# Output projections of both cross attentions as 2x2 block products with seven multiplications

## The chip, the core and the metric

The kernel runs on one core of one Trainium2 chip. Five engines work side by side, each through its own queue: TensorE (PE, with its weight loads PEld), VectorE (DVE), ScalarE (ACT), GpSimd (POOL) and SyncE (SP). The metric is the device time of one execution in microseconds; the kernel before takes 2214.82 us (median of three runs, 2214.09 to 2217.98).

## The reference

A trunk of two layers on 1024 tokens of 1024 features, float32. A layer is a token mixer (Fourier groups and neighbourhood attention in layer 0, a gated short convolution in layer 1), a cross attention into 256 memory tokens, and a gated ConvFFN. The change lies in the last line of the cross attention and in the residual addition:

```python
def memory_cross_attention(h, m, wq, wkv, wo):
    ...
    q = (h @ wq).reshape(B, S, XA_HEADS, XA_HEAD_DIM)
    ...
    p = jax.nn.softmax(s, axis=-1).astype(v.dtype)
    o = jnp.einsum('bhsm,bmhd->bshd', p, v).reshape(B, S, D)
    return o @ wo

    # in reference(), for each of the two layers, after the mixer:
    h = h + memory_cross_attention(rms_norm(h, xa_norm_g[layer]), m,
                                   xa_wq[layer], xa_wkv[layer], xa_wo[layer])
    h = h + conv_ffn(rms_norm(h, ffn_norm_g[layer]), ...)
```

## The kernel before

Activations stand transposed, features on partitions and tokens on the free axis. h is eight tiles of 128 features x 1024 tokens; chunk 0 and chunk 1 are its token halves of 512. Float32 products are made from float32r ones: an operand is split into a high part (ACT, `nc.scalar.copy`, L222) and a low part (DVE, a subtraction, L223), and `mm3` (L227 to L229) issues three matmuls into one PSUM bank. `wide_split` splits 1024 columns into two places, `half_split` 512 columns into one. SBUF is 52 places of 1024 columns and four half places of 512, handed out by `alloc`; a free half place is preferred for an allocation of 512 columns, and among free ones that which was freed longest ago.

The work is written as generators (threads) that `run` interleaves by a share of progress; each thread has a length in the call. The instruction order on each engine is fixed when the kernel is built, and need not be that of the text: what is ready early is put early.

`xattn(l, st)` is the cross attention. `qproj(c)` makes the queries of chunk c. `attn` goes over eight (chunk, head) pairs: `scores`, softmax, transposes (`turn`), then `values`, whose PSUM result is split with `half_split` into `os_`. `oproj(c)` is the output projection of chunk c through `linear`: eight blocks of 128 outputs, eight k each, weights `wo` loaded from DRAM by SP (L250) and split. `res_post` adds a block into h on DVE (L813), squares it on ACT (`sumsq`, L314) and adds up the squares on DVE (L320). The first run is `qproj(0)` alone; then `qproj(1)` and `oproj(0)` run beside `attn`; then `oproj(1)` runs alone, with `xb0` (the FFN's operands of chunk 0: `rstd`, `xnorm` L1111, `wide_split`) as a hook.

The up projection, the down projections and the convolution mixer's projections are already block products with seven multiplications. An item there is a weight block pair; of its seven weight operands three lie in DRAM as they are, and four are sums (products 7, 6, 5 and 3). `plan_sums` lists the sums to be made, and each call of `sums(src)` starts the next one of the list, whatever item it belongs to: ACT copies one element of `src` into `gates` (L1071), and POOL issues three DMAs, the gate into the target (L1072), the first operand into it (L1073), and the second one with accumulation (L1074). Each of the three writes the target and waits for the one before to land. `w_load` and `w_prep` load and split a weight operand; `plan_steps` lists them as tasks, and `ahead(n, keep)` does up to n tasks while there is room.

`down` is such a projection with a residual: products 1, 6 and 7 leave temporaries (L1474 to L1490), and product by product the results are added to or subtracted from h on DVE. CHAIN says which PSUM chain a product belongs to, OPENS and ENDS where a chain begins and ends. In `up_steps`, the FFN's operands of chunk 1 (`xb1`) follow as a background generator that `pump` moves.

The number of calls of `sums` is 136, that of sums too: 56 calls in the mixer of layer 0 (32 in its input projection, 16 and 8 in its output projections), 16 in each cross attention (four in each `qproj`, four in each `oproj`), 24 in the first up projection, 6 in the first down projection, 12 and 6 in layer 1's mixer.

Of the kernel before, what the change touches and what calls it, by code (L numbers as in the profile page):

```python
# [10 lines left out]
F32 = mybir.dt.float32  # L11
F32R = mybir.dt.float32r
AF = mybir.ActivationFunctionType
ALU = mybir.AluOpType
# [4 lines left out]
KT = 8  # L19
# [14 lines left out]
HK = 3  # L34
HU = 3
PF = 8
AW = 55.0
GATES = 64
KEEP = 8
KEEPD = 6  # L40
# [2 lines left out]
U = 512  # L43
# [85 lines left out]
class Kern:  # L129
    def __init__(self, ctx, tc, ap):  # L130
        self.tc, self.nc, self.ap = tc, tc.nc, ap
        nc = self.nc
# [25 lines left out]
        self.dr = dr  # L158
        self.q, self.did, self.op, self.xd, self.hd, self.wsrc = [], set(), {}, {}, {}, {}
        self.bg = None  # L160
        self.gates = sb.tile([P, GATES], F32, name="gates")
        self.nsum = 0

# [659 lines left out]

    def mixer0(self):
        nc = self.nc
        self.plan_sums([*self.up_items(0), *self.down_items("d0", 2, self.ap["w_down"][0]), *self.conv_items(),
                        *self.down_items("oc", 1, self.ap["w_out_c"]), *self.up_items(1),
                        *self.down_items("d1", 2, self.ap["w_down"][1])])
        self.z, self.yf, self.qkv = {}, {}, {}
        self.done = set()  # L830
# [32 lines left out]
    def xattn(self, l, st):  # L863
        nc = self.nc
        qs = [{}, {}]
        os_ = [{}, {}]
        qdone = [-1, -1]

        def qproj(c, hooks=()):
# [22 lines left out]
        def attn():  # L892
# [47 lines left out]
            def values(hd):  # L940
                h, kv, pp = hd["h"], hd["kv"], hd["p"]
                for db in range(2):
                    b = yield from self.bank(1)
                    for j in range(2):
                        self.mm3(b.f(), *self.hl(kv[1], j * NM + db * P, P), *self.wcols([pp], j * U, U),
                                 j == 0, j == 1)
                    os_[hd["c"]][2 * h + db] = yield from self.half_split(b.f())
                    self.bfree(b)
                    yield 1.3
                self.free(*pp, *kv)  # L950

            prev = nxt = ready = None
            for n in range(18):
# [20 lines left out]

        st2 = {}

        def oproj(c, hooks=()):
            psum, post = self.res_post(st2)
            while len(os_[c]) < KT:
                yield None  # L980

            def X(k, cc):
                return self.hl(os_[c][k])
            yield from self.linear([(b, c) for b in range(KT)], self.ap["wo"][l], KT, X, psum, post,
                                   hooks=hooks)
            self.free(*os_[c].values())

        self.run((qproj(0, [((0, HU), lambda: self.normed(G_XA + 8 * l, st, 1))]), 41.0))

        def main():  # L990
            yield from qproj(1)
            yield from oproj(0)
        self.run((main(), 83.0), (attn(), AW))
        self.run((oproj(1, [((0, HU), lambda: self.xb0(G_FFN + 8 * l, st2))]), 41.0))
        return st2


    def conv3(self, tmp, src, w, bias):
# [598 lines left out]
    def all(self):  # L1597
        self.run((self.warm(), 1.0))
        self.run((self.mem_load(), 1.0))

        def kv():
            yield from self.kv_thread(0)
            yield from self.kv_thread(1)
        self.run((self.x_norm(), XW), (kv(), 86.0))
        self.wfree(self.m)
        st = self.mixer0()
        self.plan_up(0)
        self.plan_down("d0", 2)
        self.plan_conv()
        self.plan_down("oc", 1)  # L1610
        st = self.xattn(0, st)
        st = self.trunk(st)
        self.plan_up(1)
        self.plan_down("d1", 2)
        st = self.xattn(1, st)
        self.last(st)
# [80 lines left out]
def prepare(x, mem, mem_norm_g, mix_norm_g, w_in_ab, rpb, w_out_ab, w_in_c, conv_c, w_out_c,  # L1697
# [18 lines left out]
    def downs(w):  # L1716
# [7 lines left out]
        "wk": np.stack([_blocks(xa_wkv[l][:, :D]) for l in range(2)]),  # L1724
        "wv": np.stack([_cols(xa_wkv[l][:, D:], 256) for l in range(2)]),
        "wq": np.stack([_blocks(xa_wq[l]) for l in range(2)]),
        "wo": np.stack([_blocks(xa_wo[l]) for l in range(2)]),
        "w_up": np.stack(up), "w_down": np.stack([downs(ffn_w_down[l]) for l in range(2)]),
        "w_cc": cc, "w_cb": cb, "w_out_c": downs(w_out_c[0]),
    }  # L1730
# [20 lines left out]
```

## Time and profile before

| | us |
|---|---|
| median of three runs | 2214.82 |
| the profiled execution, whole | 2223.45 |
| its span, first to last instruction | 2221.7 |
| PE busy | 2166.7 |
| DVE busy | 1459.9 |
| ACT busy | 960.0 |
| POOL busy | 342.4 |

Busy times are those of the profiled execution and are read against its span. PE's granted clock is 0.989 of full speed over the span. The first cross attention lies at about 460 to 675 us, the second at about 1500 to 1735 us, with the up projections right behind. A row that ends in "<-" names what ended the idle time before an instruction.

### The profile page before, as it was taken

To read this page: it belongs to the slowest core of one execution; us is meant where nothing else is said; L and a number is where in the kernel's file an instruction comes from. 1 tells how busy PE (TensorE), PEld (TensorE's weight loads), DVE (VectorE), ACT (ScalarE), POOL (GpSimd) and SP (SyncE) were. 2 spreads that over 40 slices of the span, in tenths; PEclk is the share of its full clock that TensorE was granted. 3 is DMA by queue.
4 is the path that set the end of the run, shared out by engine and by line. 5 is a ranking of instruction groups with operands and counts; after the bars stand their busy time and mean duration, and the time that the engine had idled before them with its cause. 6 is when DMAs were issued, how large, how long until landed. Compare 5 with 4: busy or idle time off the path is not lost.

```text
span 2221.7 us, 27033 instructions
## 1 busy us (share of the span) xinstructions
PE 2166.7 (98%) x10174; PEld 1788.3 (80%) x10174; DVE 1459.9 (66%) x2001; ACT 960.0 (43%) x1498; POOL 342.4 (15%) x446
## 2 busy tenths in 40 slices
PE   9999999999998999999999999999999999999998
PEld 9988888888886777777888878778888777888887
DVE  6755456666667576666767667777565757767684
ACT  6543444355445334344445223535444533334553
POOL 5222222222211221111101100011111000000002
PEclk9999999999999999999999999999999999999999
DMA  9467787789877678999874666965666635446652
GB/s 371 152 164 176 159 210 202 187 230 228 218 193 206 166 209 222 254 289 338 266 218 135 182 194 188 341 171 143 173 168 178 172 110 163 146 152 247 259 176 76
DMA packets 177891, 446.11 MB, mean 201 GB/s; under 512 B 19808, under 2 KB 87648, under 8 KB 175584
## 3 DMA queue, kind: packets, MB, share of 16 engines
q1 hardware_dynamic: 101344, 310.14, 39.6%
q0 software_dynamic: 76416, 134.25, 29.6%
q8 instruction: 79, 1.29, 0.2%
q14 instruction: 52, 0.43, 0.1%
HBM read 386.64 MB, written 191.89 MB: 260 GB/s over the span
## 4 chain that ended last, share of the span: by engine, by line
PE 81%; DMA 8%; DVE 8%; ACT 2%; issue 1%; DVEq 0%; SPq 0%; ACTq 0%
PE PS L228 27%; PE PS L227 26%; PE PS L229 26%; DMA xd_d<-p 3%; DVE p L223 2%; ACT p L222 1%; DMA p<-ws_u 1%; DMA p<-in_w_down_dram 1%; DMA xd_oc<-p 1%; PE PS L932 1%; DMA p<-in_wq_dram 1%; DVE p L1006 1%; DVE p L1008 1%; DMA p<-xd_d 0%; PE PS L695 0%
## 5 line engine op out<-in xcount | busy, mean ns | idle before, releaser
L227 PE MATMUL PS<-p,p 128*128 128x512 f32 (+1 forms) x3264 | 1225.0, 380 | 36.1 <-ACT p L222 28.4
L228 PE MATMUL PS<-p,p 128*128 128x512 f32 (+1 forms) x3264 | 1234.1, 379 | 5.1 <-DVE p L223 4.9
L229 PE MATMUL PS<-p,p 128*128 128x512 f32 (+1 forms) x3264 | 1219.5, 377 | 2.3 <-DVE p L223 2.3
L223 DVE TENSOR_TENSOR p<-p,p 128x1024 fp32r<-128x1024 f32 (+1 forms) x549 | 607.2, 1126 | 279.6 <-ACT p L222 218.9
L222 ACT CAST p<-p 128x1024 fp32r<-128x1024 f32 (+1 forms) x566 | 529.6, 959 | 571.1 <-DMA p<-xd_d 89.6
L227 PEld LDWEIGHTS PS<-p,p 128*128 128x128 f32 x3264 | 617.6, 189 | 165.9 <-ACT p L222 36.0
L228 PEld LDWEIGHTS PS<-p,p 128*128 128x128 f32 x3264 | 617.6, 189 | 125.6 <-DVE p L223 7.0
L229 PEld LDWEIGHTS PS<-p,p 128*128 128x128 f32 x3264 | 616.4, 189 | 123.3 <-DVE p L223 2.9
L314 ACT ACTIVATE p<-p 128x512 f32<-128x512 f32 (+1 forms) x128 | 74.3, 589 | 101.5 <-DVE p L813 41.8
L320 DVE TENSOR_TENSOR p<-p,p 128x512 f32<-128x512 f32 (+1 forms) x111 | 79.9, 722 | 31.4 <-ACT p L314 28.8
L223 DVE TENSOR_TENSOR p<-PS,p 128x512 fp32r<-128x512 f32 (+3 forms) x92 | 67.7, 744 | 41.3 <-ACT p L222 41.0
L1589 POOL TENSOR_TENSOR p<-p,p 128x512 f32<-128x512 f32 (+1 forms) x15 | 16.4, 1125 | 451.5 <-DVE p L494 433.7
L222 ACT CAST p<-PS 128x512 fp32r<-128x512 f32 (+3 forms) x92 | 57.3, 631 | 52.1 <-PE PS L229 28.4
L1072 POOL DMA_DIRECT2D ws_u<-gates x64 | 42.6, 756 | 241.4 <-ACT gates L1071 241.3
L813 DVE TENSOR_TENSOR p<-PS,p 128x512 f32<-128x512 f32 x64 | 43.8, 687 | 48.7 <-PE PS L229 48.7
L1005 ACT ACTIVATE p<-p,vec 128x1024 f32<-128x1024 f32 x32 | 39.7, 1242 | 66.4 <-DVE p L1305 53.6
L1006 DVE SCALAR_TENSOR_TENSOR p<-p,vec,p 128x1023 f32<-128x1023 f32 x40 | 51.2, 1281 | 20.0 <-ACT p L1005 18.4
L1074 POOL DMA_DIRECT2D ws_u<-ws_u x32 | 33.3, 1040 | 201.4 <-DMA ws_u<-in_w_up_dram 113.3
L1073 POOL DMA_DIRECT2D ws_u<-in_w_up_dram x64 | 36.9, 591 | 163.4 <-DMA ws_u<-gates 163.1
L1071 ACT COPY gates<-p 128x1 f32<-128x1 f32 x136 | 24.6, 191 | 74.1 <-DVE p L813 33.5
L1074 POOL DMA_DIRECT2D ws_u<-in_w_up_dram x32 | 33.6, 1050 | 133.7 <-DMA ws_u<-in_w_up_dram 94.9
L1300 DVE TENSOR_TENSOR p<-PS,p 128x512 f32<-128x512 f32 x32 | 22.0, 688 | 48.1 <-PE PS L229 48.0
(170 smaller groups left out, 1308.9 us busy)
## 6 DMA issues: line engine op xcount, KB each, us to landing
ws_u<-in_w_up_dram POOLq DMA_DIRECT2D x96, 512.0 KB, 5.8
p<-ws_u SPq DMA_DIRECT2D x64, 512.0 KB, 4.5
xd_d<-p SPq DMA_DIRECT2D x112, 256.0 KB, 6.0
p<-xd_d SPq DMA_DIRECT2D x56, 512.0 KB, 6.4
ws_d<-in_w_down_dram POOLq DMA_DIRECT2D x48, 512.0 KB, 6.4
p<-in_w_up_dram SPq DMA_DIRECT2D x48, 512.0 KB, 4.5
ws_u<-ws_u POOLq DMA_DIRECT2D x32, 512.0 KB, 6.2
p<-in_wq_dram SPq DMA_DIRECT2D x32, 512.0 KB, 4.5
```

What stands on the lines that cost most here:

```text
L222: self.nc.scalar.copy(hi, src)
L223: (eng or self.nc.vector).tensor_tensor(lo, src, hi.bitcast(F32), op=ALU.subtract)
L227: mm(ps, whi, xhi, start=first, stop=False, skip_group_check=True)
L228: mm(ps, whi, xlo, start=False, stop=False, skip_group_check=True)
L229: mm(ps, wlo, xhi, start=False, stop=last, skip_group_check=True)
L314: nc.scalar.activation(t.f(0, w), src, AF.Square)
L320: nc.vector.tensor_tensor(st[ch].f(0, w), st[ch].f(0, w), t.f(0, w), op=ALU.add)
L813: self.nc.vector.tensor_tensor(hc, ps, hc, op=ALU.add)
L1005: nc.scalar.activation(tmp.f(), src, AF.Identity, scale=v[:, w[1]:w[1] + 1], bias=v[:, bias:bias + 1])
L1006: nc.vector.scalar_tensor_tensor(tmp.f(1, S), src[:, 0:S - 1], v[:, w[0]:w[0] + 1], tmp.f(1, S), op0=ALU.mult, op1=ALU.add)
L1072: g.dma_start(d[0:1, 0:1], gate[0:1])
L1074: g.dma_start(d, more, accum_op=ALU.add, max_dma_last_dim=1024)
```

## The change

The output projection becomes one block product over both chunks. The 1024 x 1024 matrix `wo` and the attention's output (features by tokens) are each taken as 2 x 2 blocks of 512, and the four result blocks come from seven block products in place of eight. `values` copies its PSUM result on ACT into a raw place, two halves to a place. `o_operands` makes the seven operands from the raw places on DVE as the heads come in: operands 1 and 2 (chunk 0's blocks as they are) beside the attention, 5 and 6 with chunk 1's heads, and 7, 4 and 3 through the background generator `o_rest`. `oproj` runs in the thread of `qproj(1)`: products 1 and 2 of both couples first, then 6, 7, 4, 5, 3. The main thread's length goes from 83 to 122 and the attention's (AW) from 55 to 105.

The residual steps are those of `down`, but where `down` uses DVE to apply the temporaries of products 1, 6 and 7 to h, the new function uses `nc.gpsimd.tensor_tensor` (`pt`): twelve such steps in a layer. Two calls of `sums` stand at each of products 1, 6 and 7, one for each couple: six in a layer in place of eight. The weights of `wo` become two items per layer with four sums each; layer 0's eight are put first in the list, layer 1's ahead of the second up projection's. `xb0` starts behind product 4 of the second couple. Four hooks in `qproj(1)` load and split the first weight operands.

```diff
-AW = 55.0
+AW = 105.0
...
-        self.plan_sums([*self.up_items(0), *self.down_items("d0", 2, self.ap["w_down"][0]), *self.conv_items(),
-                        *self.down_items("oc", 1, self.ap["w_out_c"]), *self.up_items(1),
+        self.plan_sums([*self.down_items("o0", 1, self.ap["wo"][0]), *self.up_items(0), *self.down_items("d0", 2, self.ap["w_down"][0]), *self.conv_items(),
+                        *self.down_items("oc", 1, self.ap["w_out_c"]),
+                        *self.down_items("o1", 1, self.ap["wo"][1]), *self.up_items(1),
                         *self.down_items("d1", 2, self.ap["w_down"][1])])
...
-                    os_[hd["c"]][2 * h + db] = yield from self.half_split(b.f())
+                    if db == 0:
+                        r = yield from self.alloc(F32)
+                    nc.scalar.copy(r.f(db * U, (db + 1) * U), b.f())
                     self.bfree(b)
                     yield 1.3
                 self.free(*pp, *kv)
+                yield from self.o_operands(hd["c"], h, r)
...
-        def oproj(c, hooks=()):
-            psum, post = self.res_post(st2)
...
         def main():
-            yield from qproj(1)
-            yield from oproj(0)
-        self.run((main(), 83.0), (attn(), AW))
-        self.run((oproj(1, [((0, HU), lambda: self.xb0(G_FFN + 8 * l, st2))]), 41.0))
+            yield from qproj(1, [((i, 0), lambda: self.ahead(2, KEEP)) for i in (4, 5, 6, 7)])
+            yield from self.oproj("o%d" % l, st2, lambda: self.xb0(G_FFN + 8 * l, st2))
+        self.run((main(), 44.0 + 78.0), (attn(), AW))
         return st2
+
+    ORDO = ((1, 0), (2, 0), (1, 1), (2, 1)) + tuple((p, c) for p in (6, 7, 4, 5, 3) for c in range(2))
+
+    def o_operands(self, c, h, r):
+        tt = self.nc.vector.tensor_tensor
+        m = h % 2
+        half = h // 2
+        raw = self.oraw
+
+        def whole(p, x):
+            self.O.setdefault(p, []).append((yield from self.wide_split(x.f())))
+
+        if c == 0:
+            raw[half, m] = r
+            yield from whole(1 + half, r)
+        elif half == 0:
+            raw[2, m] = r
+            t1 = raw[0, m]
+            tt(t1.f(), t1.f(), r.f(), op=ALU.subtract)
+            yield from whole(5, t1)
+        else:
+            t1 = raw[0, m]
+            tt(t1.f(), r.f(), t1.f(), op=ALU.add)
+            yield from whole(6, t1)
+            raw[3, m] = r
+            if m == 1:
+                self.bg = self.o_rest()
+
+    def o_rest(self):
+        tt = self.nc.vector.tensor_tensor
+        for p, i, j in ((7, 2, 3), (4, 1, 0), (3, 3, None)):
+            for m in range(2):
+                x = self.oraw[i, m]
+                if j is not None:
+                    tt(x.f(), x.f(), self.oraw[j, m].f(), op=ALU.subtract)
+                self.O.setdefault(p, []).append((yield from self.wide_split(x.f())))
+                self.free(x)
+                if j == 0:
+                    self.free(self.oraw[0, m])
+                yield 1.0
...
+    def oproj(self, tag, st2, after):
+        nc = self.nc
+        bk, t1s, half = {}, {}, set()
+        tt, pt = nc.vector.tensor_tensor, nc.gpsimd.tensor_tensor
+
+        def done(k, c):
+            yield from self.sumsq(st2, c, k, self.hch(k, c))
+
+        def post(c, q, p, bank):
+            i, j = COUPLES[c][q]
+            b = bank.f()
+            if p == 1:
+                t1 = t1s[c, q] = yield from self.alloc(F32, 1)
+                nc.scalar.copy(t1.f(0, U), b)
+                if q == 0:
+                    self.sums(t1.f(0, 1))
+                pt(self.hch(j, 0), self.hch(j, 0), t1.f(0, U), op=ALU.subtract)
+            elif p == 6:
+                t2 = yield from self.alloc(F32, 1)
+                tt(t2.f(0, U), b, t1s[c, q].f(0, U), op=ALU.subtract)
+                if q == 0:
+                    self.sums(t2.f(0, 1))
+                pt(self.hch(i, 1), self.hch(i, 1), t2.f(0, U), op=ALU.subtract)
+                self.free(t2)
+            elif p == 7:
+                t1 = t1s.pop((c, q))
+                tt(t1.f(0, U), b, t1.f(0, U), op=ALU.subtract)
+                if q == 0:
+                    self.sums(t1.f(0, 1))
+                pt(self.hch(j, 1), self.hch(j, 1), t1.f(0, U), op=ALU.add)
+                self.free(t1)
+            elif p in (2, 4):
+                k = i if p == 2 else j
+                tt(self.hch(k, 0), b, self.hch(k, 0), op=ALU.add)
+                yield from done(k, 0)
+            elif p == 5:
+                tt(self.hch(j, 1), self.hch(j, 1), b, op=ALU.subtract)
+            else:
+                tt(self.hch(i, 1), self.hch(i, 1), b, op=ALU.add)
+                yield from done(i, 1)
+            if p in (5, 7):
+                if (c, q) in half:
+                    yield from done(j, 1)
+                half.add((c, q))
...
+            if (p, c) == (4, 1):
+                yield from self.pump()
+                self.bg = after()
+            yield from self.pump(3 if p in (5, 3) else 1)
+            yield from self.ahead(4, KEEP)
+        yield from self.pump()
...
-        "wo": np.stack([_blocks(xa_wo[l]) for l in range(2)]),
+        "wo": np.stack([downs(xa_wo[l]) for l in range(2)]),
```

## Rows read from the trace of the kernel before

**Rows 1.** The page, part 1: busy us, share of the span, instructions.

```profile
PE 2166.7 (98%) x10174; PEld 1788.3 (80%) x10174; DVE 1459.9 (66%) x2001; ACT 960.0 (43%) x1498; POOL 342.4 (15%) x446
```

**Rows 2.** Timeline of PE (start, us, instruction): first and last of twelve.

```profile
439.75 0.40 PE L227 MATMUL PS<-p,p 128*128 128x512 f32 x1
...
442.31 0.39 PE L229 MATMUL PS<-p,p 128*128 128x512 f32 x1
```

**Rows 3.** Busy time by stretch: engines with count, PE clock, DMA share, GB/s.

```profile
500.00:612.00 112.00, 112.00 (x593) 95.20 (x593) 68.96 (x119) 53.48 (x118) 25.99 (x36) 1.00 0.89 222
612.00:672.00 60.00, 60.00 (x261) 48.41 (x260) 34.56 (x44) 22.91 (x33) 10.36 (x15) 1.00 0.77 203
672.00:716.00 44.00, 37.54 (x156) 29.50 (x155) 36.46 (x38) 28.06 (x40) 7.29 (x11) 0.94 0.77 195
...
1728.00:1773.00 45.00, 41.12 (x168) 32.23 (x167) 36.99 (x38) 27.60 (x37) 3.61 (x5) 0.96 0.56 159
```

**Rows 4.** Busy time of L1071 (ACT), then of L1072 (POOL), from the start.

```profile
0.00:485.00 485.00, 10.13 (x59) 0.99 0.75 205
0.00:631.00 631.00, 11.67 (x67) 0.99 0.77 208
...
0.00:485.00 485.00, 31.88 (x43) 0.99 0.75 205
0.00:631.00 631.00, 44.75 (x59) 0.99 0.77 208
```

**Rows 5.** Timeline of POOL, layer 0's attention: sums 59, 60 and 63.

```profile
630.91 0.94 POOL L1072 DMA_DIRECT2D ws_c<-gates  x1
636.55 0.51 POOL L1073 DMA_DIRECT2D ws_c<-in_w_cc_dram  x1 [4.70 <-DMA ws_c<-gates]
641.57 1.03 POOL L1074 DMA_DIRECT2D ws_c<-in_w_cc_dram  x1 [4.51 <-DMA ws_c<-in_w_cc_dram]
642.22 0.90 POOL L1072 DMA_DIRECT2D ws_c<-gates  x1
...
682.48 0.94 POOL L1072 DMA_DIRECT2D ws_c<-gates  x1
```

**Rows 6.** Groups by line and shape, 463 to 690: busy, mean ns, idle before.

```profile
L223 DVE TENSOR_TENSOR p<-p,p 128x1024 fp32r<-128x1024 f32 x31 | 37.5, 1222 | 35.4 <-ACT p L222 29.2 <-PE PS L228 6.2
...
L813 DVE TENSOR_TENSOR p<-PS,p 128x512 f32<-128x512 f32 x16 | 11.0, 686 | 9.9 <-PE PS L229 9.9
```

**Rows 7.** Busy time by stretch, one in each up projection.

```profile
880.00:920.00 40.00, 38.54 (x167) 31.04 (x166) 24.96 (x30) 14.62 (x19) 7.73 (x11) 1.00 0.90 241
...
1938.00:1978.00 40.00, 40.00 (x174) 32.41 (x173) 26.41 (x32) 14.12 (x16) 0.00 (x0) 1.00 0.45 150
```

**Rows 8.** Groups by shape, from 2170: POOL on two operands of 512 columns.

```profile
L1589 POOL TENSOR_TENSOR p<-p,p 128x512 f32<-128x512 f32 x8 | 10.4, 1332 | 428.6 <-DVE p L494 428.6
```

**Rows 9.** Timeline of POOL, layer 1's attention: a lone sum, then two.

```profile
1669.79 0.53 POOL L1072 DMA_DIRECT2D ws_d<-gates  x1 [7.63 <-ACT gates L1071]
...
1675.52 1.03 POOL L1074 DMA_DIRECT2D ws_d<-in_w_down_dram  x1 [3.42 <-DMA ws_d<-in_w_down_dram]
1687.85 0.53 POOL L1072 DMA_DIRECT2D ws_d<-gates  x1 [11.29 <-ACT gates L1071]
...
1696.52 0.75 POOL L1072 DMA_DIRECT2D ws_d<-gates  x1
```

**Rows 10.** Timelines of ACT and DVE, from chunk 0's last Square on.

```profile
635.49 0.63 ACT L314 ACTIVATE p<-p 128x512 f32<-128x512 f32 x1 [1.17 <-DVE p L813]
...
648.39 3.49 DVE L223 TENSOR_TENSOR p<-p,p 128x1024 fp32r<-128x1024 f32 x3
...
675.58 0.56 ACT L1245 COPY p<-PS 128x512 f32<-128x512 f32 x1
```

More of the change, by code (lines that the diff above doesn't have):

```diff
@@ L160, in __init__ @@
         self.bg = None
+        self.X = {}
         self.gates = sb.tile([P, GATES], F32, name="gates")
@@ L865, in xattn @@
         qs = [{}, {}]
-        os_ = [{}, {}]
         qdone = [-1, -1]
@@ L975, in xattn @@
         st2 = {}
-        def oproj(c, hooks=()):
-            psum, post = self.res_post(st2)
[L979 to L986, printed above, removed]
+        self.O, self.oraw = {}, {}
         self.run((qproj(0, [((0, HU), lambda: self.normed(G_XA + 8 * l, st, 1))]), 41.0))
@@ new lines, in plan_o @@
+    def plan_o(self, tag):
+        self.plan_steps([((tag, c, 0), p, 2) for p, c in self.ORDO], None)
+    def oproj(self, tag, st2, after):
[40 more added lines that the diff above has]
+                half.add((c, q))
+        left = {p: 2 for p in range(1, 8)}
+        for p, c in self.ORDO:
+            key = (tag, c, 0)
+            while len(self.O.get(p, ())) < 2:
+                if self.bg is None:
+                    yield None
+                else:
+                    yield from self.pump(1)
+            yield from self.until((key, p))
+            for q in range(2):
+                ch = CHAIN[p]
+                if p in OPENS:
+                    bk[c, q, ch] = yield from self.bank(1)
+                self.product(bk[c, q, ch].f(), self.op[key, p], q, self.O[p], p in OPENS)
+                yield 2.6
+                yield from post(c, q, p, bk[c, q, ch])
+                if p in ENDS:
+                    self.bfree(bk.pop((c, q, ch)))
+            self.wdone(key, p)
+            left[p] -= 1
+            if not left[p]:
+                for x in self.O.pop(p):
+                    self.free(*x)
+            if (p, c) == (4, 1):
[4 more added lines that the diff above has]
+        yield from self.pump()
@@ L1606, in all @@
         st = self.mixer0()
+        self.plan_o("o0")
         self.plan_up(0)
@@ L1612, in all @@
         st = self.trunk(st)
+        self.plan_o("o1")
         self.plan_up(1)
```

## The prediction

> **What bounds the kernel now.** I read the page's busy times first, then PE's spacing in the timeline, then the stages, then POOL. PE is busy for 98% of the span [rows 1]. Twelve consecutive matmuls of 512 columns start 2.56 us apart from first to last, so one costs 2.56 / 11 = 0.233 us [rows 2]. Through the attention and both output projections of layer 0, PE is busy for every microsecond of the stretches 500 to 612 and 612 to 672; its first loss comes behind it, 6.5 us of the 44 from 672 on, and 3.9 us of 45 at the same place of layer 1 [rows 3]. So a matmul less is time less, as long as what feeds PE keeps up. DVE and ACT have room: 34.56 and 22.91 us of those last 60 [rows 3].
>
> The last look is at an engine that bounds nothing: POOL, which issues the weight sums. By 485 us ACT has copied 59 gates, but POOL has issued only 43 first transfers of a sum; by 631 us it is 67 against 59 [rows 4]. The 59th gate was therefore ready before 485, and POOL came to it at 630.91 [rows 5]: nearly 150 us behind. It is not busy but waits inside its queue, 4.70 us for the gate's transfer, 4.51 us for the first weight transfer [rows 5], and nothing overtakes: transfer 60, whose gate had long been copied, stands directly behind the last issue of sum 59. The kernel before doesn't feel this, as these sums are wanted hundreds of microseconds later.
>
> **The change part by part.**
>
> *Matmuls.* Before, a layer's projection has 8 blocks x 8 k x 2 chunks x 3 = 384 matmuls. After, 7 products x 2 couples x 2 blocks x 4 k x 3 = 336. That removes 48 x 0.233 = 11.2 us a layer, 22.3 us in all. All of it lies on the path where PE is full [rows 3]. One product (12 matmuls) is 2.8 us, a pair 5.6 us.
>
> *Operands.* The 16 subtractions of half width that split the attention's output go (0.69 us each); 14 splits of full width come, and 8 block sums or differences of that size. A split's DVE half is 1.22 us [rows 6]. Weight splits fall from 16 to 14. The additions into h rise from 16 to 24 on DVE at 0.69 us [rows 6]. DVE's balance for a layer is -11.0 + 14 x 1.22 + 8 x 1.22 - 2 x 1.22 + 8 x 0.69 = +19 us. It is spread over the attention stage and some 56 us behind it, where [rows 3] show 43 us idle of 112 and 25 of 60. I cost it at 0, with up to 5 us a layer when it crowds behind the attention: there the cover is the products that are left, and gone it would be a wait of the next product for a cast.
>
> *Pacing.* With AW at 105 the main thread runs more slowly beside the attention, so that some six or seven products of chunk 0 fill the attention's gaps and about twenty follow it. No row shows PE waiting there before [rows 3]; 0, with 3 us a layer as the upper end, and nothing below since there is nothing to gain.
>
> *Sums.* 16 more (136 to 152), put at the front, while the calls that start one become 2 fewer in each cross attention. Up to the end of layer 1's attention each stage makes about as many as before; 20 fall into the last up projection, which had none. Its price is the row of the same stage of layer 0, which makes them: of 40 us, PE is busy 38.54 there (DMA share 0.90) against 40.00 (0.45) [rows 7]. Over some 300 us and 20 of 24 sums that would be about 9 us; other stretches of layer 0 lose less, so I take +5, ends 0 and 9.
>
> *Twelve subtractions and additions a layer move to POOL, and this is the term that decides.* In the down projections the same residual steps for products 1, 6 and 7 are on DVE; here they are on POOL, whose queue they enter behind every sum started earlier. One costs 1.33 us there [rows 8]: 16 us a layer beside 175 us of PE, which would be nothing. But the step for the first product of layer 0 comes with the 65th sum (56 are started before the cross attention, 4 in each query projection). POOL stands at the 59th at 631 and at the 60th at 642.22 [rows 5], and nothing in the change makes it faster up to there: the same count of sums, of the same size, with the same gates.
>
> Who waits: PE's share of the attention is 96 matmuls of 512 columns, 192 of 256 at half the time and 64 transposes, about 52 us (estimate from 0.233). With one query and two output projections of 192 matmuls (44.7 us each) it fills the time up to the first up product, which starts at 672.8 (below), so the attention begins near 487. In the changed kernel 44.7 + 52 us and seven products (19.6) follow, to 603; the eighth ends near 606, products 6 and 7 (two pairs each) at 628, and product 4's first one near 631. Its addition into h on DVE must follow POOL's step of product 1. Queued behind it on DVE are the splits of operand 3, the weight splits, chunk 0's squares and the FFN's operands. ACT is caught too: product 7's temporary is one of the four half places, given back only when POOL has added it, and the next taker is the Square of product 4. So chunk 0 isn't finished before POOL has passed sum 70, and the up projection can't start before that.
>
> When is that? Between the 59th and 63rd sum POOL takes (682.48 - 630.91) / 4 = 12.9 us each, beside full DMA traffic [rows 5]. In layer 1, with light traffic, one alone takes 1675.52 + 1.03 - 1669.79 = 6.8 us, and two in a row 8.7 us [rows 9]. Once DVE stands, no place is freed and weight loads stop, so I take 9, the nearest to 8.7; ends 6.8 and 12.9. Sum 70 is then reached at 642 + 10 x 9 = 732 (710 to 771). From the last Square of chunk 0 to the second split of operand 1 it was 635.49 to 648.39 + 1.22 [rows 10], 14 us; with POOL's own two steps, 2.7 us, that is 17 us, while eight products (22 us) of 5 and 3 catch up; I take 20 (17 to 27). The first product of the up projection then starts at 752 (727 to 798). In the trace its copy starts at 675.58 [rows 10], so the product at 672.8: +79 us, saving of layer 0 included (+54 to +125).
>
> The Trainium skill's page "DMA: Bandwidth & Descriptors" (Anatomy of one DMA — SWDGE (gpsimd) path) fits 2.0 us plus bytes / 436e3 to such a transfer. By it a gate and 512 KB land in 2.0 and 3.2 us, and with the three issues a sum passes in some 7.6 us: an estimate that would put sum 70 at 718 and the total 14 us lower. The trace of the backlog disagrees, 4.70 us for the gate alone [rows 5]; the lone sum of 6.8 us agrees [rows 9].
>
> *What is late next.* In layer 1 POOL waits for gates, not for transfers, as 7.63 us ahead of 1669.79 [rows 9]: it isn't behind. Four sums in 22 us of products, at 9 us, still let it slip by some 14 us, mostly covered by products 4 and 5: +3, ends 0 and 10. The wait at the start of the first up projection (6.5 us) should shrink, since the second half of the operands has been computed while PE catches up, and fewer sums are left over for that stage: -8, ends -11 and +3.
>
> **The sum**, against the trace of 2221.7 us: +79 - 11 (layer 1) + 5 + 3 - 8 = +68. Ends: +54 - 11 + 0 + 0 - 11 = +32, and +125 - 11 + 9 + 10 + 3 and 16 us of crowding and pacing in both layers = +152. The profiled execution took 2223.45 us, 8.6 more than the median of 2214.82; I apply the difference to the median: 2283, ends 2247 and 2367. All upper ends together are unlikely.
>
> **The rivals.**
>
> *POOL is on time (the other side, faster).* If POOL's steps stood ahead of the waiting sums in its queue, or if the queue had caught up by sum 65, only the rest would count: 2214.8 - 22.3 + 5 + 2 = 2199, 2187 to 2212. It decides at one point: whether the step of product 1 has run when product 4 ends near 631; the 65th sum's gate comes near 585, so POOL may be some 46 us behind it, not the 147 of the 59th. Against it: sum 59 at 631, and the row order that lets nothing overtake [rows 5]. For it: that a step could be placed earlier among the issues than I think.
>
> *The queue drains at the lone sum's pace.* Once DVE stands, every sum may take 6.8 us as the one with nothing behind it [rows 9]; sum 70 comes at 710 then, 22 us earlier, and the time is 2261. For it: weight loads stop. Against: sums that follow at once took 8.7 or more. (The fit of the skill's page named above lies nearest to this one.)
>
> *POOL is late in layer 1 too.* There sums of 9 to 13 us meet pairs of 5.6 us; if the slip isn't covered, some 20 us more: 2303. For it: the same half places. Against: a queue that waits for gates [rows 9].
>
> *DVE, not POOL, is the limit behind the attention.* The 19 us would crowd into the 56 us there; then both layers lose 5 to 10 us, and the time is 2199 + 15 = 2214, no change. Against: 25 us idle there [rows 3].
>
> **How the numbers follow.** POOL late in layer 0 at about 9 us a sum: 0.60; at the lone sum's pace 0.18; late in layer 1 too 0.05; POOL on time 0.13; DVE the limit 0.04. I forecast 2283 us. The range takes 2245, at the lower end, and at the upper end 2325, short of all ends at once; it leaves out the case of a POOL on time and the tail. A measurement of this kernel tells about 0.2% from no change, 4.4 us. Faster: 0.13, POOL on time and a little of the last case, less its upper end; within: 0.02; slower: 0.85.
>
> **What would show it.** Right: DVE idle for tens of microseconds ahead of the first addition of product 4 of layer 0, released by POOL; POOL's steps of layer 0 between 680 and 740; PE idle for most of 640 to 740 and nowhere else by more than 10 us; the first up product near 750; layer 1's projection about 11 us shorter than before. Wrong: POOL's steps of layer 0 ahead of 640, or PE full from 500 to 660 in the changed kernel. The size goes wrong first in the time of one sum while PE stands.

## The result and the profile after

The changed kernel takes 2298.39 us (median of four runs, 2296.83 to 2307.3) against 2215.9 for the kernel before beside it: a ratio of 1.0378 (95% interval 1.0355 to 1.0400), 82 us more. The forecast was 2283, the range 2245 to 2325: slower, at a size inside the range. Its profiled execution took 2299.74 us, with a span of 2298.0. The first line of its page, which answers [rows 1], has PE 20 us less busy over a span 76 us longer:

```profile
PE 2146.4 (93%) x10078; PEld 1770.1 (77%) x10078; DVE 1503.8 (65%) x2025; ACT 992.5 (43%) x1546; POOL 413.7 (18%) x518
```

Busy time by stretch in the changed kernel (columns as in [rows 3], which the first lines answer): up to product 6 of the projection, the next 8 us, the stall, the work behind it, the start of the up projection.

```profile
500.00:628.00 128.00, 122.85 (x627) 102.98 (x626) 81.03 (x121) 69.35 (x134) 27.16 (x39) 0.97 0.82 208
628.00:636.00 8.00, 8.00 (x36) 6.46 (x35) 0.77 (x2) 1.24 (x2) 1.70 (x3) 1.00 0.70 191
636.00:730.00 94.00, 0.41 (x2) 0.00 (x0) 2.60 (x1) 0.00 (x0) 26.29 (x33) 0.52 0.52 103
730.00:780.00 50.00, 45.44 (x167) 34.59 (x168) 47.80 (x56) 25.10 (x33) 17.20 (x17) 0.88 0.86 253
780.00:920.00 140.00, 135.91 (x576) 108.64 (x575) 95.84 (x110) 59.51 (x78) 19.55 (x30) 0.99 0.55 148
```

For 94 us PE, DVE and ACT do next to nothing (0.41, 2.60 and 0.00 us), while POOL goes on with DMA issues. The granted clock is 0.52 in the stall and 0.88 in the 50 us behind it. Where [rows 3] showed every microsecond of the attention full, there are now 5 us missing before 628.

The waits of the stretch from 600 to 800 us (engine, line, what it waited for: us in total, times, the longest), the first four:

```profile
ACT p L223 <- DVE p L224: 102.3, 2, 100.6
DVE p L224 <- POOL p L1058: 98.2, 1, 98.2
PEld PS L228 <- DVE p L1055: 94.9, 1, 94.9
PE PS L228 <- DVE p L1055: 94.4, 1, 94.4
```

Read from the bottom: PE waits for a bank that DVE's subtraction of product 6 (L1055) must read; that subtraction stands on DVE behind a split (L224); the split waits for POOL's step of product 6 (L1058). The timeline of DVE around it (start, us, instruction, idle time before):

```profile
628.55 0.69 DVE L1055 TENSOR_TENSOR p<-PS,p 128x512 f32<-128x512 f32 x1 [0.48 <-PE PS L230]
...
727.40 2.79 DVE L224 TENSOR_TENSOR p<-p,p 128x1024 fp32r<-128x1024 f32 x1 [98.16 <-POOL p L1058]
730.11 0.68 DVE L1055 TENSOR_TENSOR p<-PS,p 128x512 f32<-128x512 f32 x1
```

And POOL's, which answers [rows 5]: a weight sum out of the quiet stretch and the starts of later ones, then the first residual step of product 1 and the first two of product 6.

```profile
643.31 0.94 POOL L1186 DMA_DIRECT2D ws_c<-gates  x1
648.90 0.51 POOL L1187 DMA_DIRECT2D ws_c<-in_w_cc_dram  x1 [4.64 <-DMA ws_c<-gates]
652.91 1.03 POOL L1188 DMA_DIRECT2D ws_c<-in_w_cc_dram  x1 [3.50 <-DMA ws_c<-in_w_cc_dram]
653.56 0.89 POOL L1186 DMA_DIRECT2D ws_c<-gates  x1
...
694.52 0.89 POOL L1186 DMA_DIRECT2D ws_c<-gates  x1
...
705.09 1.67 POOL L1052 TENSOR_TENSOR p<-p,p 128x512 f32<-128x512 f32 x1
...
725.71 1.66 POOL L1058 TENSOR_TENSOR p<-p,p 128x512 f32<-128x512 f32 x1
...
727.47 1.62 POOL L1058 TENSOR_TENSOR p<-p,p 128x512 f32<-128x512 f32 x1
```

From 643.31 to 694.52 there are five sums, 10.2 us each. POOL reaches the first step of product 1 at 705.09, some 120 us after ACT had its data ready. The span parts like this; the landmarks are the first copy of each up projection, the last product that its gate is multiplied into, the last gate multiplication of layer 1's convolution mixer, and the end. The differences add up to +76.3, that of the two spans; the medians differ by 82, as the profiled execution of before lay above its median. One trace stands behind each column; between two traces of one kernel (e3_spread and e11_spread_again below) such a stretch moves by up to 5 us.

| us | before | after | difference | predicted |
|---|---|---|---|---|
| to the first up copy, layer 0 | 675.6 | 783.0 | +107.4 | +79 |
| up projection, layer 0 | 339.9 | 321.2 | -18.7 | -8 |
| from there through layer 1's convolution | 401.6 | 397.6 | -4.0 | 0 |
| from there to the first up copy, layer 1 | 316.5 | 307.7 | -8.8 | -11 + 3 |
| up projection, layer 1 | 329.9 | 330.1 | +0.2 | +5 |
| to the end | 158.2 | 158.4 | +0.2 | 0 |

### The profile page after: what moved, and what is told of

Same layout as the page of the kernel before. It is cut to its first block, busy times and chain, and to the rows that moved or that the text cites. A ratio compares the mean times of both kernels' runs of the same rounds, so it can differ in the third digit from the quotient of the medians.

```text
span 2298.0 us, 27082 instructions
## 1 busy us (share of the span) xinstructions
PE 2146.4 (93%) x10078; PEld 1770.1 (77%) x10078; DVE 1503.8 (65%) x2025; ACT 992.5 (43%) x1546; POOL 413.7 (18%) x518
## 4 chain that ended last, share of the span: by engine, by line
PE 55%; DVE 7%; DMA 6%; issue 2%; ACT 2%; POOL 0%; DVEq 0%; SPq 0%; POOLq 0%; ACTq 0%
PE PS L229 18%; PE PS L230 18%; PE PS L228 18%; DVE p L224 2%; DMA xd_d<-p 2%; DMA ws_c<-gates 2%; DMA ws_c<-in_w_cc_dram 1%; DVE p L1225 1%; ACT p L223 1%; DVE p L1120 0%; DMA p<-xd_oc 0%; DVE p L321 0%; DMA p<-in_w_out_c_dram 0%; DMA xd_oc<-p 0%; ACT p L1119 0%
## 5 line engine op out<-in xcount | busy, mean ns | idle before, releaser
L228 PE MATMUL PS<-p,p 128*128 128x512 f32 (+1 forms) x3232 | 1207.9, 380 | 127.8 <-DVE p L1055 94.4
L229 PE MATMUL PS<-p,p 128*128 128x512 f32 (+1 forms) x3232 | 1220.2, 379 | 9.3 <-DVE p L224 9.1
L230 PE MATMUL PS<-p,p 128*128 128x512 f32 (+1 forms) x3232 | 1208.4, 377 | 2.6 <-DVE p L224 2.3
L224 DVE TENSOR_TENSOR p<-p,p 128x1024 fp32r<-128x1024 f32 (+1 forms) x573 | 648.6, 1152 | 352.6 <-ACT p L223 176.9
L223 ACT CAST p<-p 128x1024 fp32r<-128x1024 f32 (+1 forms) x590 | 554.3, 962 | 648.8 <-DVE p L224 135.1
L1185 ACT COPY gates<-p 128x1 f32<-128x1 f32 x152 | 27.8, 192 | 70.3 <-DVE p L814 16.7
L1414 DVE TENSOR_TENSOR p<-PS,p 128x512 f32<-128x512 f32 x32 | 22.1, 690 | 55.1 <-PE PS L230 55.1
L224 DVE TENSOR_TENSOR p<-PS,p 128x384 fp32r<-128x384 f32 (+3 forms) x60 | 46.0, 775 | 18.3 <-ACT p L223 18.1
L1423 ACT ACTIVATE p<-p 128x1024 f32<-128x1024 f32 x32 | 33.9, 1060 | 45.1 <-DVE p L1122 45.0
L224 POOL TENSOR_TENSOR p<-p,p 128x1024 fp32r<-128x1024 f32 (+1 forms) x17 | 45.4, 2684 | 42.3 <-ACT p L223 42.0
```

Of the source, the lines that this page charges most:

```text
L223: self.nc.scalar.copy(hi, src)
L224: (eng or self.nc.vector).tensor_tensor(lo, src, hi.bitcast(F32), op=ALU.subtract)
L228: mm(ps, whi, xhi, start=first, stop=False, skip_group_check=True)
L229: mm(ps, whi, xlo, start=False, stop=False, skip_group_check=True)
L230: mm(ps, wlo, xhi, start=False, stop=last, skip_group_check=True)
```

## The experiments

"First up copy" is the same landmark of layer 0 throughout. Each ratio is to the kernel before on the same chip, whose median moved between 2218 and 2222 in these runs.

**The steps on DVE (e1_dve).** It takes the suspected cause away: nothing of the residual is in POOL's queue.

```diff
-        tt, pt = nc.vector.tensor_tensor, nc.gpsimd.tensor_tensor
+        tt, pt = nc.vector.tensor_tensor, nc.vector.tensor_tensor
```

> The changed kernel with the twelve residual steps of products 1, 6 and 7 of each layer on DVE in place of POOL, nothing else. Theory A (DVE waits 98 us in layer 0 for a step that stands in POOL's queue behind late weight sums): the 94 us stall of PE at 636 is gone, the first up product's copy of layer 0 comes at about 667 (before: 675.6, changed: 783.0), and the whole is about 2201 us, 2194 to 2209, so some 15 us faster than the kernel before. The 19 us by which the first up projection got shorter in the changed kernel go back to about 340 us, as POOL is late again there. Rival B (the operands made on DVE are the limit, POOL's wait only covers it): DVE has 16 us more a layer to do here, and the time stays at 2214 or above, with PE waiting for casts and splits behind the attention. Rival C (places run short, whichever engine does the step): the wait for a place stays, 2270 or more.

Measured: 2215.46 us, ratio 0.9995 (0.9975 to 1.0015); the first up copy at 682.5. The stall is gone, so the steps on POOL were its cause; that it was the queue in front of them and not the steps themselves, e3_spread shows below. Theory A was right on the stall and wrong on the time, which is rival B's: there is no gain, though 48 matmuls a layer are saved, 22 us in both by [rows 2]. Theory A also missed the first up projection: it takes 326.2 us here and not 340. The windows of this kernel show where the 22 us went in layer 0; the second fence is the kernel before in the same stretches.

```profile
480.00:560.00 80.00, 77.08 (x423) 65.70 (x423) 48.74 (x88) 44.29 (x98) 20.75 (x30) 1.00 0.85 212
560.00:640.00 80.00, 78.19 (x368) 64.65 (x367) 64.67 (x83) 44.57 (x74) 14.61 (x20) 0.98 0.84 231
640.00:690.00 50.00, 45.73 (x177) 35.12 (x176) 38.20 (x51) 21.98 (x29) 8.34 (x12) 0.90 0.71 206
```

```profile
480.00:560.00 80.00, 79.91 (x424) 67.79 (x423) 47.24 (x82) 40.08 (x87) 20.79 (x30) 1.00 0.91 227
560.00:640.00 80.00, 80.00 (x396) 66.61 (x395) 48.71 (x75) 36.81 (x70) 16.05 (x23) 1.00 0.82 213
640.00:690.00 50.00, 50.00 (x216) 40.16 (x215) 29.71 (x40) 19.71 (x31) 8.29 (x12) 1.00 0.83 210
```

DVE (third pair) goes from 48.71 to 64.67 of 80, and PE loses 9 us of 210, part of it at a lower granted clock. This looks like the rival that the prediction gave 0.04, DVE as the limit, but the windows bear that out for half of it only: 4.3 us are lost from 640 on, behind the stretch where DVE is nearly full (56.21 of the 60 us from 600 to 660, in which PE loses nothing), and 4.7 us ahead of 580, where DVE has room.

**The steps on DVE in layer 0 alone (e2_dve_layer0).** Layer 1 keeps POOL, where the queue was not behind.

```diff
-        tt, pt = nc.vector.tensor_tensor, nc.gpsimd.tensor_tensor
+        tt, pt = nc.vector.tensor_tensor, (nc.vector if tag == "o0" else nc.gpsimd).tensor_tensor
```

> The changed kernel with the twelve steps on DVE in layer 0 alone; in layer 1 they stay on POOL. Theory A: layer 0's stall is gone, and in layer 1, where POOL waits for gates and not for transfers, POOL's steps cost 0 to 5 us: the time is within 5 us of that of the kernel with all steps on DVE, about 2203. Rival (a step on POOL costs by itself, by its own time or by keeping DVE out of SBUF): some 10 us or more above that kernel.

Measured: 2209.4 us, ratio 0.9958 (0.9939 to 0.9976), faster than e1_dve beside it by 0.3%, 6 us, where theory A had said within 5. From the end of the convolution to layer 1's first up copy it is 312.1 us against 318.1 in e1_dve. The windows of layer 1 at the same times, e1_dve first and then this kernel, which comes to its first up copy 5 us later:

```profile
1590.00:1720.00 130.00, 123.84 (x585) 101.43 (x584) 104.87 (x139) 70.98 (x114) 16.77 (x24) 0.99 0.66 194
```

```profile
1590.00:1720.00 130.00, 129.07 (x626) 106.99 (x625) 102.48 (x129) 73.70 (x122) 36.61 (x36) 1.00 0.67 195
```

PE is busy for 5 us more when POOL has the steps; counted from the end of the convolution to each kernel's own first up copy, it loses 9.5 us of 312 in place of 13.1 of 318. One trace could be chance, but the others agree: with layer 1's steps on POOL the stretch takes 307.8 us in the change and 311.7 to 312.2 in e3_spread, e11_spread_again and e9_half, with the steps on DVE 318.1 and, in e7_spread_dve, 323.1. POOL is the better engine for them where its queue is short.

**Fewer sums ahead of them (e3_spread, e11_spread_again).** The steps stay on POOL, but of layer 0's mixer the 16 calls in the first output projection start no sum, and product 5 of the up projections and of layer 1's convolution mixer (its weight blocks of two) starts one more. So from sum 33 on the list comes 16 calls later up to the first up projection.

```diff
-            if st is None or b % 2 == 1:
+            if st is not None and b % 2 == 1:
                 self.sums(hc[:, 0:1])
...
-                if q == 0 and nq == 2 and p in (1, 6, 7):
+                if q == 0 and nq == 2 and p in (1, 6, 7, 5):
                     self.sums(self.mark)
```

> The changed kernel with its twelve steps a layer still on POOL, but with fewer sums started ahead of the first cross attention: the 16 calls in the first half of layer 0's output projection start none, and the up and convolution stages start one more for each of their weight blocks of two (at product 5), so that the same 152 sums are made, 40 in place of 56 ahead of the attention. POOL reached sum 43 at 485 us in the kernel before, so it should be at most some 20 us behind here. Theory A: the steps run within 20 us of their temporaries, no stall over 10 us in layer 0, 2200 to 2215 us. Rival (the steps on POOL are the cost, not what stands ahead of them): 2280 or more.

> The kernel of e3_spread once more (steps on POOL, 16 weight sums moved from layer 0's front to the up projections), on another chip and beside e10_rest_pool. If its gain is real, the ratio to the kernel before is 0.990 to 0.996 again; if it was the chip's, it is 0.998 to 1.002.

Measured: 2204.34 us, ratio 0.9929 (0.9901 to 0.9958), and on another occasion 2211.2 us, 0.9965 (0.9948 to 0.9983). Both intervals lie below 1 and overlap; the gain is 0.4 to 0.7%. As e2_dve_layer0, at 0.9958, lies between the two, neither version is clearly the fastest. Theory A holds: from 480 to 690 us PE waits for 1.0 us at most at a time. The first up copy comes at 674.5 (671.6 in the second one). POOL's timeline of e3_spread has the steps at their time, 103 to 123 us earlier than in the change (the first steps of products 1 and 6, the last of product 7):

```profile
582.22 1.69 POOL L1052 TENSOR_TENSOR p<-p,p 128x512 f32<-128x512 f32 x1
...
622.44 1.30 POOL L1058 TENSOR_TENSOR p<-p,p 128x512 f32<-128x512 f32 x1 [10.10 <-issue]
...
641.10 2.21 POOL L1065 TENSOR_TENSOR p<-p,p 128x512 f32<-128x512 f32 x1 [2.44 <-DVE p L1062]
```

**Half the dose (e9_half).** Only 8 of the 16 calls are left out, with no call added.

```diff
-            if st is None or b % 2 == 1:
+            if b % 2 == 1:
```

> The changed kernel with 8 of its 16 weight sums of the output convolution dropped from layer 0's front (every second one), the steps on POOL as in the change. It asks for the dose. Theory A (POOL's in-order queue, 10.3 us a sum when it is behind): POOL's lag when the attention begins falls by 8 x 10.3 = 82 us, from 160 to about 75 to 80; its step for product 6, at 725 us in the changed kernel, comes near 643, and the first copy of layer 0's up projection, 783 there and 674.5 without the 16 sums, near 690 (685 to 705). Time 2212 to 2230. Theory T (a threshold: any sum ahead of the steps costs about the same wait, such as the gate's round trip, or the stall is from something else in POOL's steps): first copy at 740 or later, or at 675; time over 2260 or at 2204.

Measured: 2264.59 us, ratio 1.0197 (1.0165 to 1.0229); first up copy at 734.1. Half of the sums bring back 49 of the 108.5 us that lie between the change and e3_spread: no threshold, as theory A said. But its size was wrong, 734 against 685 to 705. The same waits as in the change, shorter:

```profile
ACT p L223 <- DVE p L224: 64.8, 5, 59.5
DVE p L224 <- POOL p L1058: 57.0, 1, 57.0
PEld PS L228 <- DVE p L1055: 53.7, 1, 53.7
PE PS L228 <- DVE p L1055: 53.3, 1, 53.3
```

POOL's step of product 6 starts at 679.14 in place of 725.71, 46.6 us for eight sums, 5.8 us each and not 10.3. Both traces, between the gates of sums 33 and 56, show why: the changed kernel goes from 410.26 to 598.90, 8.2 us a sum; e9_half from 414.31 to 648.07, 10.2 us. In the changed kernel the gate of the next sum is issued ahead of a sum's own accumulating transfer in all 23 cases (486.85 and 487.90 are two such gates), so that the transfers of two sums overlap; in e9_half in 14 of 23. So a call left out lets the queue shrink by less than a sum's lone time, since those that remain overlap less. Why POOL's order differs wasn't followed: gates lay ready for about 60 us or more in both. The ratio gives back less than the landmark, 40% (1.0378 in the change, 1.0197 here, 0.9929 in e3_spread), and so the time lies in theory T's range: the last stretch takes 173.7 us in place of 158.4, and the last four sums lie in it, where the change has none.

**The place of product 6's temporary (e4_place).** The prediction named product 4's addition as the first to wait; the trace showed a split whose place had been that temporary. Here these places are given back only at the end.

```diff
-                self.free(t2)
+                t2s.append(t2)
...
+        self.free(*t2s)
```

> The changed kernel, in which product 6's temporaries keep their places to the end of the projection, so that no split has to wait until POOL has read one. In the changed kernel DVE's 98 us were such a wait: the output place of a split was product 6's temporary. Theory A: POOL is as late as before, so DVE or ACT only wait a little later, at product 4's addition into h (it needs POOL's step of product 1, near 705) and at the places of product 7's temporaries: the first wait begins some 10 to 20 us later, and the whole is 2275 to 2300. Rival C (the reuse of these places is the whole fault): 2200 to 2215.

Measured: 2290.15 us in one run; first up copy at 768.1. The waits from 600 to 800 us (lines from L1185 on are one higher here):

```profile
DVE p L1062 <- POOL p L1052: 74.5, 2, 68.9
...
PE PS L228 <- DVE p L1062: 65.9, 2, 63.6
...
ACT p L315 <- POOL p L1065: 16.5, 2, 15.4
```

The first wait moves to the next instruction that needs POOL: product 7's subtraction (L1062) writes the temporary of product 1 in place, which POOL has still to read. Behind it comes the Square that takes a half place of product 7, as the prediction had it. Theory A holds, with a first wait that begins 5 us later and not 10 to 20. The first up copy comes 15 us earlier than in the change, of 108.5 that the stall costs; the total, from one run with a granted clock of 0.98 in layer 1, says less. With POOL that late, one waiter follows another, and which one is first is worth little.

**What in e3_spread counts (e7_spread_dve).** The calls as in e3_spread, the steps on DVE as in e1_dve.

> As e3_spread (16 weight sums of layer 0 moved to the up projection), but the steps on DVE as in e1_dve. It parts the two things that e3_spread has over e1_dve (11 us in the time). Theory D (DVE is full behind the attention, 70 of 80 us in e1_dve, and POOL's taking the steps off it is the gain): the tail of layer 0 keeps e1_dve's gaps and half clock, 2210 to 2216. Theory S (what helps is that fewer weight sums stand ahead of the weights and of the rest of POOL's work): 2201 to 2207, as e3_spread.

Measured: 2223.13 us, ratio 1.0010 (0.9995 to 1.0024), like e1_dve and not like e3_spread, though above theory D's range. Moving the sums has no worth of its own; taking the steps from DVE has, and the sums must be out of the way for that. From 640 to 690 us PE loses 5.26 us here and 1.50 in e3_spread. But DVE isn't less busy in e3_spread (68.04 of the 80 us from 560 on, 66.47 here), as its splits take longer there (below); so which of DVE's instructions come earlier for it isn't shown.

**More of DVE's work to POOL (e10_rest_pool).** As e3_spread, with the four full-width subtractions per layer that make the operands of products 7 and 4 on POOL.

```diff
     def o_rest(self):
-        tt = self.nc.vector.tensor_tensor
+        tt = self.nc.gpsimd.tensor_tensor
```

> As e3_spread, and the four subtractions a layer that make the operands of products 7 and 4 (full width, 1.21 us each on DVE) are on POOL too. Theory D (DVE's work behind the attention is what limits there): 4.9 us a layer less for DVE, and the time is 2 to 6 us below e3_spread. Theory E (POOL's latency and the shared operands): a subtraction costs POOL about 2 x 1.33 = 2.7 us, the split behind it waits for it and DVE's own splits are held up meanwhile, so it is 2 to 10 us above e3_spread.

Measured: 2234.78 us, ratio 1.0061 (1.0040 to 1.0082), about 1% above e11_spread_again, which ran beside it. Theory E held, and more than it said. Groups by line and shape from 560 to 640 us (count, busy us, mean ns, idle before): the splits from SBUF in e1_dve, in e11_spread_again with its four subtractions, and in this kernel.

```profile
L224 DVE TENSOR_TENSOR p<-p,p 128x1024 fp32r<-128x1024 f32 x25 | 30.1, 1215 | 7.1 <-ACT p L223 6.7 <-PE PS L230 0.4
```

```profile
L224 DVE TENSOR_TENSOR p<-p,p 128x1024 fp32r<-128x1024 f32 x28 | 37.9, 1370 | 2.8 <-ACT p L223 2.0 <-PE PS L230 0.4 <-POOL p L1058 0.3
...
L1025 DVE TENSOR_TENSOR p<-p,p 128x1024 f32<-128x1024 f32 x4 | 4.8, 1211 | 0.0
```

```profile
L224 DVE TENSOR_TENSOR p<-p,p 128x1024 fp32r<-128x1024 f32 x26 | 48.3, 1881 | 2.9 <-ACT p L223 2.3 <-PE PS L230 0.4
...
L224 DVE TENSOR_TENSOR p<-PS,p 128x1024 fp32r<-128x1024 f32 x4 | 4.9, 1216 | 0.5 <-ACT p L223 0.5
```

DVE gives up 4.8 us and gets back 10.4, though two splits fewer lie in the window: the same split takes 1215 ns on the mean with no step on POOL, 1370 with twelve half-width ones in the window, 1881 with ten of them and four full-width ones (3.37 us each on POOL by their own group). The splits with a PSUM operand stay at 1216; one of the four ran wholly beside a POOL step, in 1.21 us.

**The pace (e5_aw80, e6_aw92, e8_aw118).** e3_spread with another length of the attention, AW; the change has 105.

> As e3_spread (16 weight sums of layer 0 moved to the up projection, steps on POOL), with the attention's share of the planner's turn, AW, back from 105 to 80, which is about the ratio of attention to main work of the kernel before. In doubt is what the projection's products cost while they run beside the attention. Theory P (pacing): AW 105 with the products' splits crowds DVE and ACT, so that TensorE shows gaps of about 1 us and a half clock after them (7 us in layer 0's attention of e1_dve); at 80 the attention runs without gaps, and 4 to 7 us a layer come back: 2190 to 2198, first copy of layer 0's up projection at 668 to 671. Theory C (cover): with 80 the main thread reaches product 6 before the attention has made its operand and has nothing else to give, so that the attention's last part runs uncovered; TensorE waits there and the time is 2206 to 2225, first copy after 676.

> As e5_aw80 with AW 92, halfway. Theory P: 2195 to 2202, about half of the gain of AW 80. Theory C: 2204 to 2212, about half of its loss. If both work, this one lies below both e3_spread (2204) and e5_aw80.

> As e3_spread with AW 118 in place of 105: the attention gets a larger share of the planner's turns still, and fewer products stand beside it. AW 80 and 92 lost 36 and 21 us against e3_spread on the same scale, since the products in front ran out of operands; this run looks past 105. Theory C (cover ends last on that side only): the loss was from too many products in front, 118 has more behind the attention, so it is within 4 us of e3_spread, 2200 to 2208. Theory P (the gaps of about 1 us in the front of the attention, from 502 to 548 us, come from too little beside it): they grow at 118, TensorE loses 3 to 8 us more from 480 to 560, and the time is 2208 to 2216.

| AW (105: trace of e3_spread) | ratio to before | first up copy, us | PE busy of 80, 480 to 560 | of 80, 560 to 640 | of 50, 640 to 690 |
|---|---|---|---|---|---|
| 80 | 1.0090 (1.0060 to 1.0119) | 691.1 | 80.00 | 74.15 | 41.67 |
| 92 | 1.0024 (1.0008 to 1.0039) | 685.9 | 80.00 | 76.30 | 45.14 |
| 105 | 0.9929 and 0.9965 | 674.5 | 77.69 | 79.62 | 48.50 |
| 118 | 1.0059 (1.0039 to 1.0079) | 682.0 | 79.62 | 77.76 | 42.29 |

Theory P fell: the gaps ahead of 560 do vanish at 80, as it said, but more is lost behind, and at 118 they shrink as well. Theory C had the sign below 105, though both lost more than it said, and was wrong above it. The largest single wait of PE from 590 to 690 us is of one kind at both ends of the table, AW 80 and then AW 118:

```profile
PE PS L331 <- DVE p L321: 4.9, 1, 4.9
```

```profile
PE PS L331 <- DVE p L321: 6.5, 1, 6.5
```

That is the sum of squares ahead of the up projection: DVE is late at the end of chunk 0, whichever side the work is pushed to. How the loss above 105 arises in detail wasn't followed.

## Why the prediction was right, and where it was not

*POOL is late in layer 0, and DVE, ACT and PE stand behind it: right.* The steps ran at 705 to 749 us (predicted 680 to 740), PE stood from 636 to 730, and DVE was idle for tens of microseconds, released by POOL. Taking the steps from POOL (e1_dve) or the sums from in front of them (e3_spread) removes all of it, half the sums 45% of it. The lag was as read from [rows 4] and [rows 5]: 150 us before, 160 after.

*Its size: +107 in place of +79, and one term of the sum is the cause.* The release came at 727.4, where sum 70 was put at 732. That it fits so well is luck: POOL came to sum 60 at 653.56 and not at 642, a sum in the quiet took 10.2 us and not 9, but the release needed only sum 66, not 70. What was mis-sized is the time from there to the first up product: 20 us (17 to 27) in the forecast, 53 in the trace, from 727 to the product of the copy at 782.96. The prediction let the wait begin at product 4's addition, with eight products left. It began at product 6, since a split had been given that product's temporary as its place and DVE keeps its order; so products 7 and 4 stood behind it too. PE had 167 matmuls left, the count of its row from 730 to 780: fourteen products, 39 us by [rows 2], where the forecast had eight and 22. The rest went at a granted clock of 0.88 in that row and with DVE busy for 47.80 of its 50 us. e4_place shows that the next waiter would have come some 5 us later, at 634, and that it too stands ahead of product 4's addition.

*The whole is nearer than its parts, and that is luck too.* The first stretch came out 28 us above its forecast, the others together 20 us below theirs, so that the spans differ by 76 us where 68 was forecast.

*Layer 1's projection: right.* -8.8 against -11 + 3. POOL wasn't behind there.

*Layer 0's saving of 11 us: right as arithmetic, not seen in the time.* With the stall removed (e3_spread), the first up copy comes at 674.5, 1 us before that of the kernel before (4 us in e11_spread_again). PE loses 4.1 of 210 us from 480 to 690 there, in the attention's front and behind it; the rest of the 11 us could not be placed, since the traces lack some matmul records.

*DVE's crowding at 0 to 5 us a layer: at its upper end.* With the steps on POOL and no stall (e3_spread) PE loses 4.1 us more than before in layer 0. With the twelve steps on DVE too (e1_dve) it is 9 in layer 0 and 6 in layer 1, beyond the term. That e1_dve's 2215 equals the 2214 of the rival "DVE is the limit" is partly luck, as the rival had no such steps on DVE. "25 us idle of 60" was an average: DVE is busy for 56.21 of the 60 us from 600 on in e1_dve. The rival of a POOL on time, 2199 (2187 to 2212), is the case of e3_spread, and its price was good: its two ratios, on the 2214.82 of the kernel before, are 2199 and 2207.

*The other rivals.* "At the lone sum's pace" falls, 10.2 us in place of 6.8, with PE, DVE and ACT at rest. "Late in layer 1 too" falls by layer 1's -8.8.

*The start of the up projection: -8 forecast, -18.7 measured, and -4.0 in the stretch after it.* PE's busy time shows the lost part going from 16.7 us of 341 to 4.7 of 321, while the DMA share fell from 0.81 to 0.69. POOL had worked through its sums in the stall, but that can be only part of it: without a stall the stretch is shorter too, by 13.8 us in e1_dve (DMA share 0.80), 10.4 in e3_spread and 8.0 in e11_spread_again. So the forecast of -8 fits a kernel without the stall, and 5 to 11 us go with the stall; that the fewer transfers give them is not shown. The other 7 us of the stretch are a difference in busy time that I can't assign.

*The 20 sums in the last up projection: +5 forecast, +0.2 measured.* The price came from layer 0's row of a DMA share of 0.90 [rows 7]; no cost of the sums shows there beyond what a stretch moves by from trace to trace.

*The fit for a POOL transfer.* By the Trainium skill's page "DMA: Bandwidth & Descriptors" (Anatomy of one DMA — SWDGE (gpsimd) path) a sum would pass in some 7.6 us, an estimate. In the quiet stretch that is too low by a quarter: a sum took 10.2 us there, the gate alone 4.5 to 4.9 us, as in the backlog.

## What to carry to other kernels

An engine that is 15% busy can be the worst place for a step: what counts is not its load but how far its queue is behind, and this is read from the time between a sum's trigger and its issue. Before work is moved to a queue that waits inside itself, move the waits out of its way, or leave the work where it was; half of the waits removed gave 45% of the stall back. When work goes from DVE to POOL, look at the durations of what remains on DVE, not at the count.

## What the runs showed of the hardware that I had not expected

POOL's and DVE's operations on two SBUF operands hold each other up. In the changed kernel a split that usually takes 1.22 us takes 2.79 (the line of 727.40 above) beside POOL's step of 727.47, which lasts 1.62; DVE's subtractions with one operand in PSUM (L1055, L1062) stay at 0.68 us next to such steps. In e3_spread the 23 splits from SBUF that overlap a step of the two projections take 1.62 us on the mean. POOL's step in turn is stretched from 1.3 to as much as 2.2 us where a split is already under way, and then the split keeps its own time, as here in e3_spread:

```profile
632.23 1.21 DVE L224 TENSOR_TENSOR p<-p,p 128x1024 fp32r<-128x1024 f32 x1
632.39 2.22 POOL L1065 TENSOR_TENSOR p<-p,p 128x512 f32<-128x512 f32 x1 [0.30 <-DVE p L1062]
```

The Trainium skill's page "GPSIMD Engine Reference" (section 1, Specifications) names this contention for DVE instructions with two SBUF inputs. The runs agree with it. They also give its size here: the split of 727.40 lost about the whole duration of the step beside it, and e10_rest_pool took 4.8 us from DVE and cost it 10.4.

A gate's transfer, one element, that is issued directly behind an accumulating one takes 4.5 to 4.9 us to land even with PE, DVE and ACT at rest, and so the three dependent transfers of a sum cost POOL 10.2 us there; in [rows 9] a lone sum took 6.8. Two lines of the changed kernel's POOL show a gate with no transfer in front of it, which landed 1.3 us after its issue had ended:

```profile
784.08 0.54 POOL L1186 DMA_DIRECT2D ws_c<-gates  x1 [12.93 <-ACT gates L1185]
785.94 0.52 POOL L1187 DMA_DIRECT2D ws_c<-in_w_cc_dram  x1 [1.32 <-DMA ws_c<-gates]
```

What the gate waits for seems to be the accumulating transfer: issued 0.6 us behind it (642.67 and 643.31) or 1.9 us behind it (704.42 and 706.30), the gate landed 6.2 us after that transfer's issue both times.
